# An encoder block on one core: the second half of its last gate as one product of 1024 columns, three of its eight pieces by seven products

## The chip, the cores and the metric

The kernel runs on 1 core of one Trainium2 chip. The metric is the device time of one execution in microseconds (us); the time of a kernel is the median of its runs. Before the change three runs took 1457.73, 1457.87 and 1458.08 us.

## The reference, cut to what matters

The program is one layer of an encoder on 256 tokens of 2048 features, all in float32: a combined input projection, two kinds of attention, gates, an output projection, a gated MLP, and at the end an embedding `p` (256 x 256) that is projected and gated by the residual. The change touches the last three lines:

```python
    x = x + (jax.nn.gelu(g) * (hf @ w_ffn_up[i])) @ w_ffn_down[i]
    gate_p = jax.nn.sigmoid(rms_norm(x, ple_norm[i]) @ w_ple_gate[i])   # 2048 x 2048
    x = x + gate_p * (p[i] @ w_ple_proj[i])
    return rms_norm(x, final_norm)
```

The result is 256 x 2048. The last norm needs the sum of squares over all 2048 columns of a token before any of its columns can be scaled and written.

## The kernel before, in words

**Products in three parts.** Each float32 operand is held as a rounded part ("hi", type float32r) and a remainder ("lo"). One product of a 128 x 128 block of activations with 128 rows x 512 columns of weights is three matmuls, hi·hi, hi·lo and lo·hi (`thirds`, L361, lines L364 to L366), summed in one PSUM bank. PE (TensorE) does them; the activations are the stationary side.

**Pieces.** All weights come as pieces of 1 MB (128 x 2048 elements) in the order in which PE will use them; the table `_PIECES` is written once by `_pieces` (L109). SP (SyncE) loads them in that order into 3 buffers (`load`, L240). `produce` (L246) turns a piece into units: ACT (ScalarE) copies hi from the raw weights (L263), DVE (VectorE) subtracts to get lo (L264). hi and lo units lie in rings of buffers, 6 for plain units ("u") and 2 for summed ones ("v", L184); a unit is made when a ring has a buffer free, that is when PE has used up an older one.

**Two ways to use a piece.** A piece of a 1024-column product holds two rows of blocks (k and k+1) by two column groups of 512; with the two halves of the tokens (t = 0, 1) that is a 2 x 2 times 2 x 2 block product. Kind "s" takes it by 8 products (24 matmuls) in two units of 1024 columns. Kind "S" takes it by 7 products (21 matmuls), into the banks M1, M7, M5, M6, M2, M3, M4. For that it needs sums of the activations (`combos`, tiles S, made once and kept) and of the weights: DVE writes three differences into the raw piece (L256 on 1024 columns, L257 and L258 on 512), and the piece becomes four units: 512 and 1024 plain columns (u) and two of 1024 summed columns (v; T13 from the first half of the raw piece, T24 from the second). Before the last piece of such a stage, `row_sums` (L803) combines M1, M6, M7 and M5 into two tiles c0 and c1 (one copy on ACT, L810, and four adds on DVE, L811 to L814); each finished output bank (M2, M3, M4, P22) is then added to them by DVE.

**The end of the program.** After the MLP's last product (stage F11) come pp0 and pp1 (`p` times its weights, kept in the tile `last`), then the last gate in three stages. G0 is its first 1024 columns: eight pieces in the pattern "SsSsSsSs" (`ALT`); its outputs go through `first_rows` and `ple` (L1077, L1068): add c, tanh on ACT (L1071), times the projection (DVE, L1072), plus the residual xr (DVE, L1073), square with a row sum (ACT, L1074), times the norm's weights (DVE, L1075). G2 and G3 are the third and fourth 512 columns, each by `wide_stage` (L421): four pieces by 8 products, in two accumulators, one for each half of the tokens. In G3 the last two pieces are joined, first all products of t = 0, then all of t = 1, so that the rows of t = 0 are finished and written while PE works on t = 1. What follows the last matmul is in L1091 to L1110: on halves of 256 columns tanh (L1094), times the projection (L1095), plus the residual (L1096), square (L1097); then the row sum (L1099, L1100), its power -1/2 on POOL (GpSimd, L1102), the norm's weights (L1103), the scaling of four column groups (L1109 on DVE, L1107 on ACT) and the transfer of each (L1110).

The norm's weights `gains` (1 MB, L1035) are loaded by SP right after the MLP in the program's order.

**What sets the order.** The kernel is written in program order with steps that fall due at a place (stage, piece, product). A scheduling layer then writes one fixed order for each engine; each engine runs its own in that order and waits on semaphores. Buffers are handed on in the order in which they are asked for.

Of the kernel before, what the change touches and what calls it, by code (L numbers as in the profile page):

```python
# [12 lines left out]
AF = mybir.ActivationFunctionType  # L13
# [4 lines left out]
T = 256  # L18
# [75 lines left out]
ALT = "SsSsSsSs"  # L94
DOWN = "SsSsSsSsSss"
FIRST_GATES = "ssssSsSs"


def _ffn(half):
# [10 lines left out]
def _pieces():  # L110
# [77 lines left out]
def _encoder(ctx: ExitStack, tc, xt, pt, xrow, cols, gainrow, table, onehot, mask, ident_in, wts, out):  # L188
# [92 lines left out]
    def drop(u):  # L281
        del made[u]
        state["u" if _UNITS[u][1] == "n" else "v"] += 1
        pump()
# [518 lines left out]
    def row_sums(stage, last, finish):  # L803

        names = ("M2", "M3", "M4", "P22")

# [17 lines left out]
    def quads(stage, moving, combos, finish):  # L824
        last = len(_STAGES[stage]) - 1
        row_sums(stage, last, finish)
        quad_stage(stage, moving, combos)
        run_due(stage, last, 8)

    def sums_of(u, tag):  # L830

# [203 lines left out]
    nc.sync.dma_start(gains, gainrow)  # L1035
    for pair, which in enumerate(("M2", "M3", "M4", "P22")):
        at(("pp0", 0, 4 + pair), rows_pair, which, 4 + pair, pl, 2)

# [41 lines left out]
        ple(t, n, c, c)  # L1080

    quads("G0", lambda k: pl[:, k, :], lambda i: combos["pl", i], first_rows)
    c = outputs()
    for a, t in zip(wide_stage("G2", lambda k: pl[:, k, :], ("M1", "M7")), range(2)):
        ple(t, 2, a, c[t][:, cut[0]])
    accs = wide_stage("G3", lambda k: pl[:, k, :], ("M5", "M6"), 2)
    known = sc.tile([P, 2], F32, name="known", bufs=1)
    nc.vector.tensor_reduce(known, ssq[:, :, :3], axis=AX.X, op=ALU.add)
    nc.vector.tensor_scalar(known, known, D * EPS, None, op0=ALU.add)
    for t in range(2):  # L1090
        for h in range(2):  # L1091
            cols = slice(3 * WIDE + h * T, 3 * WIDE + (h + 1) * T)
            u, r = c[t][:, WIDE + h * T:WIDE + (h + 1) * T], xr[:, t, cols]
            nc.scalar.activation(u, accs[t][:, h * T:(h + 1) * T], AF.Tanh, scale=held["rp"][:, t:t + 1])  # L1094
            nc.vector.scalar_tensor_tensor(u, u, 1.0, ph[:, t, cols], op0=ALU.add, op1=ALU.mult)  # L1095
            nc.vector.tensor_tensor(r, r, u, op=ALU.add)  # L1096
            nc.scalar.activation(u, r, AF.Square, accum_out=ssq[:, t, 3 + h:4 + h])  # L1097
        v = sc.tile([P, 1], F32, name="v3")
        nc.vector.tensor_tensor(known[:, t:t + 1], known[:, t:t + 1], ssq[:, t, 3:4], op=ALU.add)  # L1099
        nc.vector.tensor_scalar(v, ssq[:, t, 4:], known[:, t:t + 1], 1.0 / D, op0=ALU.add, op1=ALU.mult)  # L1100
        r = sc.tile([P, 1], F32, name="r3")
        nc.gpsimd.tensor_tensor(r, v, mhalf[:, :1], op=ALU.pow)  # L1102
        nc.vector.tensor_tensor(xr[:, t, cut[3]], xr[:, t, cut[3]], gains[:, cut[3]], op=ALU.mult)  # L1103
        for n in range(4):
            row = xr[:, t, cut[n]]
            if n == 1:
                nc.scalar.activation(row, row, AF.Copy, scale=r)  # L1107
            else:
                nc.vector.tensor_scalar(row, row, r, None, op0=ALU.mult)  # L1109
# [55 lines left out]
```

## Time and profile before

| what | us |
|---|---|
| median of three runs | 1457.87 |
| the profiled execution | 1458.43 |
| its span | 1456.6 |
| PE busy | 1445.2 |
| DVE busy | 1248.2 |
| ACT busy | 824.1 |

The span is that of the profiler, and the profiled execution took 1.83 us more than its span; it lies 0.56 us above the median. Engines are named as above; a DMA that SP or ACT starts is listed under SPq or ACTq. A matmul's shown length (0.39 us at 512 columns) is longer than the step from one to the next, because matmuls overlap; the step is what counts. In a row of the order in time the number in brackets is how long the engine had been idle, and for whom.

### The profile page before, as it was taken

How to read it: one execution, taken by the hardware profiler on the slowest of the kernel's cores; microseconds unless marked ns; L12 is line 12 of the kernel's file. 1: busy time of each engine (PE TensorE's matmuls, PEld its weight loads, DVE VectorE, ACT ScalarE, POOL GpSimd, SP SyncE). 2: the span in 40 equal slices, each digit the busy share in tenths (PEclk: the TensorE clock that was granted, in tenths of full speed). 3: DMA queues.
4: the chain of work that ended last, by engine and by line, in shares of the span. 5: the costliest groups of instructions: out<-in, count | busy, mean ns of one | idle time of the engine just before them, and what ended most of it. 6: DMA issues, size and time to landing. Idle time of an engine off the chain costs nothing.

```text
span 1456.6 us, 19524 instructions
## 1 busy us (share of the span) xinstructions
PE 1445.2 (99%) x7488; PEld 1237.1 (85%) x7488; DVE 1248.2 (86%) x1841; ACT 824.1 (57%) x1149; POOL 4.9 (0%) x9
## 2 busy tenths in 40 slices
PE   9999999999999999999999999999999999999997
PEld 8888888888888888888888888888888888888785
DVE  7777665679998989989888899989888889999994
ACT  7555544546555656566555555455555555565763
POOL 0000000000000000000000000000000000000000
PEclk9999999999999999999999999999999999999999
DMA  9764445435456456465554545465555554546462
GB/s 319 259 205 152 148 170 175 174 143 202 187 192 233 185 204 238 177 231 190 188 200 175 202 149 224 173 257 182 201 181 195 182 195 172 191 193 249 156 233 85
DMA packets 46456, 282.88 MB, mean 194 GB/s; under 512 B 5076, under 2 KB 9812, under 8 KB 14108
## 3 DMA queue, kind: packets, MB, share of 16 engines
q1 hardware_dynamic: 45500, 280.46, 52.7%
q8 instruction: 58, 0.95, 0.3%
q10 hardware_dynamic: 864, 1.19, 0.2%
q14 instruction: 34, 0.28, 0.1%
HBM read 279.49 MB, written 2.14 MB: 193 GB/s over the span
## 4 chain that ended last, share of the span: by engine, by line
PE 98%; ACT 1%; issue 0%; DMA 0%; DVE 0%; POOLq 0%; POOL 0%; ACTq 0%; DVEq 0%
PE bank L307 29%; PE bank L314 15%; PE bank L364 14%; PE bank L365 14%; PE bank L366 14%; PE bank L291 2%; PE bank L353 2%; PE bank L355 2%; PE bank L354 2%; PE bank L292 1%; PE bank L858 1%; PE bank L675 0%; PE bank L623 0%; PE bank L622 0%; PE bank L621 0%
## 5 line engine op out<-in xcount | busy, mean ns | idle before, releaser
L263 ACT ACTIVATE uh<-raw 128x1024 fp32r<-128x1024 f32 (+2 forms) x518 | 522.1, 1017 | 402.2 <-PE bank L307 183.4
L264 DVE TENSOR_TENSOR ul<-raw,uh 128x1024 fp32r<-128x1024 f32 (+2 forms) x518 | 596.6, 1169 | 134.1 <-ACT uh L263 70.3
L307 PE MATMUL bank<-hf,uh 128*128 128x512 f32 x1408 | 336.4, 391 | 0.0
L307 PEld LDWEIGHTS bank<-hf,uh 128*128 128x128 f32 x1408 | 258.9, 188 | 50.2
L314 PEld LDWEIGHTS bank<-hf,ul 128*128 128x128 f32 x1408 | 180.4, 191 | 6.7
L314 PE MATMUL bank<-hf,ul 128*128 128x256 f32 x1408 | 182.8, 283 | 0.0
L263 ACT ACTIVATE vh<-raw 128x1024 fp32r<-128x1024 f32 x92 | 97.4, 1059 | 55.7 <-DVE raw L256 27.9
L264 DVE TENSOR_TENSOR vl<-raw,vh 128x1024 fp32r<-128x1024 f32 x92 | 111.8, 1218 | 0.4
L307 PE MATMUL bank<-hs,uh 128*128 128x512 f32 x432 | 103.6, 392 | 0.0
L445 ACT ACTIVATE t<-bank 128x256 f32<-128x256 f32 x122 | 46.5, 384 | 95.1 <-PE bank L314 89.7
L307 PEld LDWEIGHTS bank<-hs,uh 128*128 128x128 f32 x432 | 79.5, 188 | 15.6
L364 PE MATMUL bank<-uh,act 128*128 128x512 f32 x232 | 90.4, 390 | 0.0
L365 PE MATMUL bank<-ul,act 128*128 128x512 f32 x232 | 90.4, 390 | 0.0
L366 PE MATMUL bank<-uh,act 128*128 128x512 f32 x232 | 90.3, 389 | 0.0
L364 PE MATMUL bank<-uh,hs 128*128 128x512 f32 x172 | 67.3, 391 | 0.0
L366 PE MATMUL bank<-uh,hs 128*128 128x512 f32 x172 | 67.2, 391 | 0.0
L365 PE MATMUL bank<-ul,hs 128*128 128x512 f32 x172 | 67.1, 390 | 0.0
L256 DVE TENSOR_TENSOR raw<-raw 128x1024 f32<-128x1024 f32 x46 | 56.1, 1220 | 0.6
L314 PE MATMUL bank<-hs,ul 128*128 128x256 f32 x432 | 56.6, 284 | 0.0
L314 PEld LDWEIGHTS bank<-hs,ul 128*128 128x128 f32 x432 | 54.5, 191 | 1.0
L364 PE MATMUL bank<-vh,S 128*128 128x512 f32 x138 | 54.3, 398 | 0.0
L365 PE MATMUL bank<-vl,S 128*128 128x512 f32 x138 | 54.1, 392 | 0.0
(240 smaller groups left out, 2275.1 us busy)
## 6 DMA issues: line engine op xcount, KB each, us to landing
raw<-in_wts SPq DMA_DIRECT2D x251, 1024.0 KB, 4.8
raw<-in_wts SPq DMA_DIRECT2D x12, 512.0 KB, 7.3
xr<-in_xrow SPq DMA_DIRECT2D x4, 512.0 KB, 9.5
x<-in_xt SPq DMA_DIRECT2D x13, 128.0 KB, 6.5
hb<-hold SPq DMA_DIRECT2D x3, 514.0 KB, 7.5
hb<-hold SPq DMA_DIRECT2D x2, 768.0 KB, 7.4
last<-in_gainrow SPq DMA_DIRECT2D x1, 1024.0 KB, 4.9
out<-xr SPq DMA_DIRECT2D x4, 256.0 KB, 2.6
```

The lines of the kernel that those rows point to most:

```text
L256: nc.vector.tensor_tensor(raw[:, :2 * WIDE], raw[:, WIDE:3 * WIDE], raw[:, :2 * WIDE], op=ALU.subtract)
L263: nc.scalar.activation(hi, src, AF.Copy)
L264: nc.vector.tensor_tensor(lo, src, hi.bitcast(F32), op=ALU.subtract)
L291: nc.tensor.matmul(acc, hi[:, w], m, start=first, stop=False, skip_group_check=True)
L307: nc.tensor.matmul(acc, weights(u)[0][:, o * P:(o + 1) * P], m, start=first, stop=False, skip_group_check=True)
L314: nc.tensor.matmul(acc[:, T:], weights(u)[1][:, o * P:(o + 1) * P], m[:, :T], start=False, stop=last, skip_group_check=True)
L353: nc.tensor.matmul(acc[:, :n * P], xh, hi, start=(k == 0), stop=False)
L354: nc.tensor.matmul(acc[:, :n * P], xh, lo, start=False, stop=False)
L364: nc.tensor.matmul(acc, sh, wh, start=first, stop=False)
L365: nc.tensor.matmul(acc, sh, wl, start=False, stop=False)
L366: nc.tensor.matmul(acc, sl, wh, start=False, stop=last)
L445: keep(nc.scalar.activation(t, acc[:, T:], AF.Copy, scale=scale))
```

## The change

G2 and G3 become one stage G2 over the last 1024 columns, in eight pieces of the pattern `LAST = "SsSsSsss"`: pieces 0, 2 and 4 (counted from 0) by seven products, the others by eight. The sums of the activations for pieces 0, 2 and 4 are those that G0 made. The last two pieces are joined: PE takes them output by output, (t, n) = (0,0), (0,1), (1,0), (1,1), with 12 matmuls for each, n being the column group. The combining of M1, M6, M7 and M5 falls due one piece earlier, at piece 5.

Each output goes through `last_rows` when its bank is done: add c (DVE, L1101), tanh (ACT, L1102), times the projection (DVE, L1103), plus the residual (DVE, L1104), square (ACT, L1106). The last output, (1,1), is taken in two halves of 256 columns. When n = 1 is done, the row's power is formed and the row of that t is scaled and written. For t = 0 two column groups are scaled by ACT (L1125), and two by DVE with the norm's weights in the same instruction (L1129), where there were a multiplication (L1103) and three scalings on DVE before.

The load of `gains` moves from behind the MLP to the first product of G0. On SP it stood behind the load of F11's last piece and now stands after that of G0's piece 4, seven loads later.

```diff
+LAST = "SsSsSsss"
...
-    for s in (2, 3):
-        wide("G%d" % s, ("w_ple_gate", s * WIDE), KC)
+    quads("G2", ("w_ple_gate", 2 * WIDE), ("w_ple_gate", 3 * WIDE), LAST)
...
-    def quad_stage(stage, moving, combos=None, tags=("M2", "M3", "M4", "P22")):
+    def quad_stage(stage, moving, combos=None, tags=("M2", "M3", "M4", "P22"), joint=1):
...
-        for i, p in enumerate(pieces):
+        alone = len(pieces) - joint if joint > 1 else len(pieces)
+        for i, p in enumerate(pieces[:alone]):
...
+        rest = [(i, c) for i in range(alone, len(pieces)) for c in range(2)]
+        for g, (t, n, i, c) in enumerate((t, n, i, c) for t in range(2) for n in range(2) for i, c in rest):
+            run_due(stage, alone, g)
+            w = cut(_UNITS_OF[pieces[i]][c], n if c == 0 else 1 - n)
+            put(tags[2 * t + n], part(moving(2 * i + c), t), w)
+        for i, c in rest:
+            drop(_UNITS_OF[pieces[i]][c])
...
-        at((stage, last, 0), first)
+        at((stage, last, 0) if joint == 1 else (stage, last - 1, 0), first)
         for t in range(2):
             for n in range(2):
-                at((stage, last, 2 * (2 * t + n + 1)), end, t, n)
+                at((stage, last, 2 * joint * (2 * t + n + 1)), end, t, n)
...
-    nc.sync.dma_start(gains, gainrow)
+    at(("G0", 0, 0), lambda: keep(nc.sync.dma_start(gains, gainrow)))
...
+    def last_rows(t, n, a):
+
+        end = 3 * WIDE if n else 2 * WIDE
+        step = T if t and n else WIDE
+        for h in range(WIDE // step):
+            cols = slice(end + h * step, end + (h + 1) * step)
+            u, r = held["c"][t][:, cols.start - 2 * WIDE:cols.stop - 2 * WIDE], xr[:, t, cols]
+            nc.vector.tensor_tensor(u, a[:, h * step:(h + 1) * step], u, op=ALU.add)
+            nc.scalar.activation(u, u, AF.Tanh, scale=held["rp"][:, t:t + 1])
             nc.vector.scalar_tensor_tensor(u, u, 1.0, ph[:, t, cols], op0=ALU.add, op1=ALU.mult)
             nc.vector.tensor_tensor(r, r, u, op=ALU.add)
-            nc.scalar.activation(u, r, AF.Square, accum_out=ssq[:, t, 3 + h:4 + h])
+            e = 2 + n + h
+            nc.scalar.activation(u, r, AF.Square, accum_out=ssq[:, t, e:e + 1])
+        k = known[:, t:t + 1]
+        if not n:
+            nc.vector.tensor_reduce(k, ssq[:, t, :3], axis=AX.X, op=ALU.add)
+            nc.vector.tensor_scalar(k, k, D * EPS, None, op0=ALU.add)
+            if t:
+                nc.vector.tensor_tensor(xr[:, t, cut[2]], xr[:, t, cut[2]], gains[:, cut[2]], op=ALU.mult)
+            return
         v = sc.tile([P, 1], F32, name="v3")
...
+        for m in range(4):
+            row = xr[:, t, cut[m]]
+            if m == 1 or not (t or m):
                 nc.scalar.activation(row, row, AF.Copy, scale=r)
+            elif t or m < 2:
+                nc.vector.tensor_scalar(row, row, r, None, op0=ALU.mult)
             else:
-                nc.vector.tensor_scalar(row, row, r, None, op0=ALU.mult)
-            (nc.scalar if n % 2 else nc.sync).dma_start(out[:, t, cut[n]], row)
+                nc.vector.scalar_tensor_tensor(row, row, r, gains[:, cut[m]], op0=ALU.mult, op1=ALU.mult)
+            (nc.scalar if m % 2 else nc.sync).dma_start(out[:, t, cut[m]], row)
+
+    quads("G2", lambda k: pl[:, k, :], lambda i: combos["pl", i], last_rows, 2)
```

Three places in the engines' orders show what this moves. The first is DVE where it makes the third piece of the stage after G0 (raw_12679 in both kernels). Before, the rows stand among the last steps for G0's outputs, and all the lo units (ul) are of plain weights:

```order
L1073 TENSOR_TENSOR xr_4920<-xr_4920,c_12721 128x512
L264 TENSOR_TENSOR ul_12772<-raw_12679,uh_12771 128x1024
L1075 TENSOR_TENSOR xr_4920<-xr_4920,last_12302 128x512
L264 TENSOR_TENSOR ul_12776<-raw_12679,uh_12775 128x1024
L1079 TENSOR_TENSOR c_12721<-bank_12520,c_12721 128x512
L264 TENSOR_TENSOR ul_12810<-raw_12692,uh_12809 128x1024
L264 TENSOR_TENSOR ul_12820<-raw_12692,uh_12819 128x1024
L1072 SCALAR_TENSOR_TENSOR c_12721<-c_12721,last_12302 128x512
```

Now, on the same engine from the second plain unit of that piece (ul_12787) to its last summed unit (vl_12833):

```order
L264 TENSOR_TENSOR ul_12787<-raw_12679,uh_12786 128x1024
L1083 TENSOR_TENSOR xr_4920<-xr_4920,last_12302 128x512 x2
L1087 TENSOR_TENSOR c_12732<-bank_12520,c_12732 128x512
L256 TENSOR_TENSOR raw_12679<-raw_12679 128x1024
L1080 SCALAR_TENSOR_TENSOR c_12732<-c_12732,last_12302 128x512
L257 TENSOR_TENSOR raw_12679<-raw_12679 128x512
L1081 TENSOR_TENSOR xr_4920<-xr_4920,c_12732 128x512
L258 TENSOR_TENSOR raw_12679<-raw_12679 128x512
L264 TENSOR_TENSOR vl_12813<-raw_12679,vh_12812 128x1024
L1083 TENSOR_TENSOR xr_4920<-xr_4920,last_12302 128x512
L264 TENSOR_TENSOR vl_12833<-raw_12679,vh_12832 128x1024
```

The three differences and the two summed units of the piece now stand between the steps for G0's last output. From the lo half of the first unit of G0's last piece (ul_12648, which stands at the same place in both orders) to vl_12833 DVE has 39 instructions: 13 of 1024 columns and 26 of 512.

The second place is DVE at the end of the program. Before, from the first use of the rows' power of t = 0 (r3_13053) the rows of t = 1 follow by themselves:

```order
L1109 TENSOR_SCALAR xr_4920<-xr_4920,r3_13053 128x512 x3
L1095 SCALAR_TENSOR_TENSOR c_12786<-c_12786,last_12302 128x256 x2
L1096 TENSOR_TENSOR xr_4920<-xr_4920,c_12786 128x256 x2
L1099 TENSOR_TENSOR known_13039<-known_13039,ssq3_12442 128x1
L1100 TENSOR_SCALAR v3_13072<-ssq3_12442,known_13039 128x1
L1103 TENSOR_TENSOR xr_4920<-xr_4920,last_12302 128x512
L1109 TENSOR_SCALAR xr_4920<-xr_4920,r3_13075 128x512 x3
```

Now, from the add of output (1,0) (bank_12828) to the first instruction for the last output's halves after tanh (bank_12864 is the last output):

```order
L1101 TENSOR_TENSOR c_12985<-bank_12828,c_12985 128x512
L1117 TENSOR_SCALAR v3_13051<-ssq3_12441,known_12796 128x1
L1129 SCALAR_TENSOR_TENSOR xr_4920<-xr_4920,r3_13053,last_12302 128x512 x2
L1103 SCALAR_TENSOR_TENSOR c_12985<-c_12985,last_12302 128x512
L1101 TENSOR_TENSOR c_12985<-bank_12864,c_12985 128x256
L1104 TENSOR_TENSOR xr_4920<-xr_4920,c_12985 128x512
L1101 TENSOR_TENSOR c_12985<-bank_12864,c_12985 128x256
L1109 TENSOR_REDUCE known_12796<-ssq3_12441 128x1
L1112 TENSOR_TENSOR xr_4920<-xr_4920,last_12302 128x512
L1110 TENSOR_SCALAR known_12796<-known_12796 128x1
L1103 SCALAR_TENSOR_TENSOR c_12985<-c_12985,last_12302 128x256 x2
L1104 TENSOR_TENSOR xr_4920<-xr_4920,c_12985 128x256 x2
```

The scaling of t = 0 and most of output (1,0) now stand ahead of the add of the last output.

The third place is ACT there, where c_12985 is the tile of t = 1. Before:

```order
L1107 ACTIVATE xr_4920<-xr_4920,r3_13053 128x512
L1110 DMA out_0<-xr_4920 128x512 x2
L1094 ACTIVATE c_12786<-bank_12934,rh_12388 128x256 x2
L1097 ACTIVATE c_12786,ssq3_12442<-xr_4920 128x256 x2
L1107 ACTIVATE xr_4920<-xr_4920,r3_13075 128x512
```

Now:

```order
L1102 ACTIVATE c_12985<-c_12985,rh_12387 128x512
L1125 ACTIVATE xr_4920<-xr_4920,r3_13053 128x512 x2
L1130 DMA out_0<-xr_4920 128x512 x2
L1106 ACTIVATE c_12985,ssq3_12441<-xr_4920 128x512
L1102 ACTIVATE c_12985<-c_12985,rh_12387 128x256 x2
L1106 ACTIVATE c_12985,ssq3_12441<-xr_4920 128x256 x2
L1125 ACTIVATE xr_4920<-xr_4920,r3_13108 128x512
```

The square of output (1,0) stands ahead of the last output's tanh.

More of the change, by code (lines that the diff above doesn't have):

```diff
@@ L801, in outputs, with row_sums @@
         return held["c"]
-    def row_sums(stage, last, finish):
+    def row_sums(stage, last, finish, joint=1):
         names = ("M2", "M3", "M4", "P22")
@@ L817, in end, with quads @@
             finish(t, n, held["accs"][names[2 * t + n]])
-        at((stage, last, 0), first)
+        at((stage, last, 0) if joint == 1 else (stage, last - 1, 0), first)
         for t in range(2):
             for n in range(2):
-                at((stage, last, 2 * (2 * t + n + 1)), end, t, n)
[L824 to L828, printed above, removed]
+                at((stage, last, 2 * joint * (2 * t + n + 1)), end, t, n)
+    def quads(stage, moving, combos, finish, joint=1):
+        last = len(_STAGES[stage]) - joint
+        row_sums(stage, last, finish, joint)
+        quad_stage(stage, moving, combos, joint=joint)
+        run_due(stage, last, 8 * joint)
     def sums_of(u, tag):
@@ L1082, in _encoder @@
     quads("G0", lambda k: pl[:, k, :], lambda i: combos["pl", i], first_rows)
[L1083 to L1086, printed above, removed]
     known = sc.tile([P, 2], F32, name="known", bufs=1)
[L1088 to L1094, printed above, removed]
+    def last_rows(t, n, a):
[6 more added lines that the diff above has]
+            nc.scalar.activation(u, u, AF.Tanh, scale=held["rp"][:, t:t + 1])
@@ L1098, in _encoder @@
         v = sc.tile([P, 1], F32, name="v3")
-        nc.vector.tensor_tensor(known[:, t:t + 1], known[:, t:t + 1], ssq[:, t, 3:4], op=ALU.add)
-        nc.vector.tensor_scalar(v, ssq[:, t, 4:], known[:, t:t + 1], 1.0 / D, op0=ALU.add, op1=ALU.mult)
+        if t:
+            nc.vector.tensor_tensor(k, k, ssq[:, t, 3:4], op=ALU.add)
+        nc.vector.tensor_scalar(v, ssq[:, t, 3 + t:4 + t], k, 1.0 / D, op0=ALU.add, op1=ALU.mult)
         r = sc.tile([P, 1], F32, name="r3")
         nc.gpsimd.tensor_tensor(r, v, mhalf[:, :1], op=ALU.pow)
-        nc.vector.tensor_tensor(xr[:, t, cut[3]], xr[:, t, cut[3]], gains[:, cut[3]], op=ALU.mult)
@@ L1104, in _encoder @@
-        for n in range(4):
-            row = xr[:, t, cut[n]]
-            if n == 1:
+        if t:
+            nc.vector.tensor_tensor(xr[:, t, cut[3]], xr[:, t, cut[3]], gains[:, cut[3]], op=ALU.mult)
+        for m in range(4):
+            row = xr[:, t, cut[m]]
+            if m == 1 or not (t or m):
                 nc.scalar.activation(row, row, AF.Copy, scale=r)
-            else:
-                nc.vector.tensor_scalar(row, row, r, None, op0=ALU.mult)
-            (nc.scalar if n % 2 else nc.sync).dma_start(out[:, t, cut[n]], row)
+            elif t or m < 2:
+                nc.vector.tensor_scalar(row, row, r, None, op0=ALU.mult)
+            else:
+                nc.vector.scalar_tensor_tensor(row, row, r, gains[:, cut[m]], op0=ALU.mult, op1=ALU.mult)
+            (nc.scalar if m % 2 else nc.sync).dma_start(out[:, t, cut[m]], row)
```

## The prediction

> **What bounds the kernel now.** I read the page first, then the busy time by stages.
>
> ```profile
> span 1456.6 us, 19524 instructions
> PE 1445.2 (99%) x7488; PEld 1237.1 (85%) x7488; DVE 1248.2 (86%) x1841; ACT 824.1 (57%) x1149; POOL 4.9 (0%) x9
> PE 98%; ACT 1%; issue 0%; DMA 0%; DVE 0%; POOLq 0%; POOL 0%; ACTq 0%; DVEq 0%
> ```
>
> PE is the bound over the whole: fewer matmuls are worth their time, if PE is not made to wait. Whether it will is read from the stages. The rows are G0, then G2 with G3, then what follows the last matmul.
>
> ```profile
> core 0: us, PE busy (x) PEld busy (x) DVE busy (x) ACT busy (x) POOL busy (x), PEclk, DMA share, GB/s
> 1362.20:1403.00 40.80, 40.80 (x180) 33.44 (x179) 40.07 (x55) 24.08 (x30) 1.07 (x1) 1.00 0.56 214
> 1403.00:1446.95 43.95, 43.95 (x194) 36.04 (x193) 31.26 (x46) 21.99 (x37) 0.93 (x1) 1.00 0.29 105
> 1446.95:1456.60 9.65, 0.00 (x0) 0.00 (x0) 3.71 (x10) 2.47 (x7) 0.93 (x1) 0.68 0.57 211
> ```
>
> In G0, where every second piece goes by seven products, DVE is busy for 40.07 of 40.80 us: it only just keeps up. In G2 and G3 it has 12.7 us to spare, and the change puts DVE work there. In the waits from 1300 us on PE has one, for the copy of a pp output:
>
> ```profile
> PE bank L364 <- ACT last L1059: 0.6, 1, 0.6
> ```
>
> **PE's own work.** 49 matmuls in a row, the first and the last of them:
>
> ```profile
> 1435.68 0.39 PE L366 MATMUL bank<-uh,pl 128*128 128x512 f32 x1
> ...
> 1446.56 0.39 PE L366 MATMUL bank<-uh,pl 128*128 128x512 f32 x1
> ```
>
> One step is (1446.56 − 1435.68)/48 = 0.227 us. Three pieces by 21 matmuls in place of 24 save 9 x 0.227 = 2.04 us. From 1403.0 the 183 matmuls would put the start of the last one at 1444.5 instead of 1446.56.
>
> **The load of the norm's weights.** Before, SP held the following loads behind it; the rows are SP's wait, and then ACT and DVE without raw weights.
>
> ```profile
> SPq L1035 <- PE bank L366: 6.3, 1, 6.3
> ...
> 1340.67 2.01 ACT L263 ACTIVATE uh<-raw 128x1024 fp32r<-128x1024 f32 x2 [6.05 <-DMA raw<-in_wts]
> ...
> 1341.77 2.36 DVE L264 TENSOR_TENSOR ul<-raw,uh 128x1024 fp32r<-128x1024 f32 x2 [2.37 <-ACT uh L263]
> ```
>
> At its new place, behind the load of G0's piece 4, its buffer has long been free, and its first use (L1083) is over 30 us later; the loads behind it wait for DVE to empty a buffer anyway, so it costs nothing there. Freed of the 6.3 us, DVE starts the pp pieces earlier, by 0 to 2.4 us; the six u buffers, which PE empties, will take part of that back, and I take 1.0. PE's 0.6 us should mostly go too.
>
> **DVE's work at the hand-over from G0.** A piece by seven products needs three differences and 3584 columns of lo in place of 2048. The queue's price for 512 and 1024 columns:
>
> ```profile
> 1375.76 0.68 DVE L850 TENSOR_TENSOR pair<-pl 128x512 f32<-128x512 f32 x1
> 1376.36 0.68 DVE L264 TENSOR_TENSOR ul<-raw,uh 128x512 fp32r<-128x512 f32 x1
> ...
> 1391.85 1.22 DVE L264 TENSOR_TENSOR ul<-raw,uh 128x1024 fp32r<-128x1024 f32 x1
> 1392.98 1.22 DVE L264 TENSOR_TENSOR vl<-raw,vh 128x1024 fp32r<-128x1024 f32 x1
> 1394.12 3.52 DVE L264 TENSOR_TENSOR ul<-raw,uh 128x1024 fp32r<-128x1024 f32 x3
> ```
>
> From start to start 0.60 and 1.14 us, the last one of a chain its full 1.22. The differences add 1.14 + 2 x 0.60, the lo units (0.60 + 3 x 1.14) − 2 x 1.14 = 1.74: 4.1 us more for each of three pieces. The first of them meets the outputs of G0, on which DVE spends 16 instructions of 512 columns and four for the combining, none of which G0's own start had beside it.
>
> The row at 1391.85 is ul_12648, where the quoted order starts counting. From there to the end of vl_12833 stand 26 of 512 and 13 of 1024 columns: 26 x 0.60 + 12 x 1.14 + 1.22 = 30.5 us, so 1422.35 without a gap, and 1421.35 with the 1.0 us above. PE reaches vl_12833 in the third piece; from its first use to the end it has 117 matmuls. The last starts at 1421.4 + 116 x 0.227 = 1447.7. Until piece 4 the sums stay level: vl_12894 is ready at 1430.2 and wanted at 1430.25, so each gap of DVE (where it waits for a copy or a square of ACT) goes straight to the end. I add 0.4 for these, with bounds 0 and 1. The start of the last matmul moves from 1446.56 to 1448.1, **+1.5 us** (bounds +0.4 and +2.7). So of the 2.04 us nothing is left, and PE waits some 4 us in all, most of it in the third piece for the units made after L256 to L258 (about 2 us at one place, since the square of an output also stands ahead of the last hi copy on ACT).
>
> Here a rule bears on the price. The Trainium skill, "VectorE: DVE Perf Modes", section "The DRAIN you can't avoid", says that the next operation does not start until the pipe has emptied, which I read as: each costs its whole duration. Then the 39 would take 26 x 0.68 + 13 x 1.22 = 33.5 us and the end would be 3.0 us later. The rows above show starts 0.08 us before the predecessor's end, so the sum goes by 0.60 and 1.14.
>
> **The end of the program.** The rows are those of t = 0 and t = 1 before, with one square and one tanh of 512 columns from G2.
>
> ```profile
> 1406.58 0.61 ACT L1074 ACTIVATE c<-xr 128x512 f32<-128x512 f32 x1
> 1407.10 0.19 ACT L1074 ACTIVATION_READ_ACCUMULATOR c<-xr 128x1 f32 x1
> ...
> 1414.00 0.71 ACT L1071 ACTIVATE c<-c,rh 128x512 f32<-128x512 f32 x1
> ...
> 1441.12 0.39 PE L366 MATMUL bank<-uh,pl 128*128 128x512 f32 x1
> ...
> 1441.54 0.84 ACT L1094 ACTIVATE c<-bank,rh 128x256 f32<-128x256 f32 x2 [9.59 <-PE bank L366]
> ...
> 1444.15 0.21 DVE L1100 TENSOR_SCALAR v<-ssq,known 128x1 f32<-128x1 f32 x1 [0.24 <-ACT c L1097]
> 1444.45 0.93 POOL L1102 TENSOR_TENSOR r<-v,mhalf 128x1 f32<-128x1 f32 x1 [78.33 <-DVE v L1100]
> 1445.41 1.28 DVE L1109 TENSOR_SCALAR xr<-xr,r 128x512 f32<-128x512 f32 x3 [0.44 <-POOL r L1102]
> 1447.12 0.84 ACT L1094 ACTIVATE c<-bank,rh 128x256 f32<-128x256 f32 x2 [0.98 <-PE bank L366]
> 1447.62 0.79 DVE L1095 SCALAR_TENSOR_TENSOR c<-c,last 128x256 f32<-128x256 f32 x2 [0.94 <-ACT c L1094]
> ```
>
> Call L the start of the last matmul (1446.56). A bank is read 0.42 us after its last matmul starts (1441.12 to 1441.54), and from the row sum to its use is 1.26 us (1444.15 to 1445.41). Before, the last rows' product (L1095) starts at L + 1.06. Now output (0,1) is done 24 matmuls before the last: DVE adds at L − 5.0, tanh runs until L − 3.6, product and sum on DVE until L − 2.1 (the row sum of (0,0) in between waits for its square), its square until L − 1.25, the row sum starts at L − 1.2, and the power is there at about L. The new wait is that of L1129 for it. Behind it in DVE's queue stand the product and the sum of (1,0) and the add of the last output: L1129 twice until L + 1.25, product to 1.85, add of a half (0.35) to 2.2, sum of (1,0) ends at 2.9. Then ACT squares (1,0) until 3.65, before the last tanh; DVE waits for that row sum, multiplies by the norm's weights (0.60), and starts the last output's products at L + 4.45. From there the work is that of before (two products, two sums, two squares, power, four scalings, transfers). So the end grows by 4.45 − 1.06, **+3.4 us**. If L1129 did not wait, the add could come at L + 0.45 and the products at L + 3.1: at least +2.0; at most +4.0, with 0.6 more for gaps. I take 3.3.
>
> **The sum.** +1.5 + 3.3 = +4.8 us. In the profiled execution's own time 1458.43 + 4.8 = 1463.2; that execution lies 0.56 above the median, so the median becomes 1457.87 + 4.8 = 1462.7. The bounds add up to +2.4 and +6.7.
>
> **Rivals.** First, DVE keeps up. If freeing SP lets DVE run ahead by 4 us or more instead of 1.0, every summed unit is there when PE wants it. Then PE ends 2.04 + 0.6 us earlier, the end still grows by 3.3, and the time is 1458.5: not slower. For it speaks ACT, which in G0 is busy 24.08 of 40.80 us; against it DVE's 40.07 and the two v buffers, which let no summed unit be made more than one piece ahead. 0.14.
>
> Second, the clock. The waits of the third piece lie close together, and a long enough rest takes the clock down. The rows are after the last matmul:
>
> ```profile
> 1449.00:1450.00 1.00, 0.00 (x0) 0.00 (x0) 0.52 (x4) 0.69 (x4) 0.00 (x0) 1.00 0.53 201
> 1450.00:1451.00 1.00, 0.00 (x0) 0.00 (x0) 0.55 (x2) 0.01 (x1) 0.93 (x1) 0.67 0.00 0
> 1451.00:1452.00 1.00, 0.00 (x0) 0.00 (x0) 1.00 (x3) 0.71 (x1) 0.00 (x0) 0.50 0.00 0
> ```
>
> Some 3.5 us after PE's last work the granted clock is 0.50. If PE's 2 us grow to that, matmuls take 0.45 us for as long again: about 8 of them, 1.8 us, plus 1.5 of the longer wait, 1466.0. The Trainium skill, "TensorE: Matmul & The Clock Gate", section "Why this matters for your kernels", asks for no gap over about 3 us; the rows above agree with that size. 0.05.
>
> Third, the full pipe of the rule above: 3.0 us more, 1465.7. The rows speak against it. 0.03.
>
> **How the numbers follow.** The forecast has 0.78 (1460.3 to 1464.6 by its bounds). 0.2% is 2.9 us, about what a measurement of this kernel can tell from no change, so slower begins at 1460.8. Slower: 0.73 of the forecast and 0.08 of the last two, 0.81. Within 0.2%: 0.05 from its low end and 0.11 of the first rival, 0.16. Faster: 0.03, the first rival with a short end as well. The range of 1459.6 to 1465.2 leaves out most of the first rival at one side and the other two at the other.
>
> **What would show it.** In the new profile: no wait of 6.3 us on SP, DVE idle less than 2.37 us before the pp pieces, and PE's 0.6 us gone or smaller; DVE without a gap from G0's last pieces until about 1422; waits of PE of about 4 us on the v units in the third piece of the new stage; the last matmul starting at 1447 to 1449; L1129 starting at about L, the last L1103 at L + 4.45, and 13.4 us from L to the end of the span, against 10.0. I would be wrong if PE shows no wait in the new stage, or if the last tanh comes within 1 us of the last matmul.

## The result, and the profile after

| | before | after |
|---|---|---|
| median, us (6 runs each) | 1457.97 | 1463.73 |
| from, to | 1457.73 to 1458.43 | 1462.41 to 1464.74 |
| the profiled execution | 1458.43 | 1462.41 |
| its span | 1456.6 | 1460.6 |

The ratio is 1.0039, with a 95% interval of 1.0026 to 1.0052: the change makes the kernel slower by 5.76 us in the medians. The profiled execution of after is the fastest of its six, so its span shows less of the loss (4.0 us) than the medians do; where the rest comes from took experiments. Line numbers below are those of each kernel's own text; the edits shift them a little.

The page of after, in the same three lines as before:

```profile
span 1460.6 us, 19532 instructions
...
PE 1443.3 (99%) x7479; PEld 1233.3 (84%) x7479; DVE 1264.2 (87%) x1861; ACT 830.6 (57%) x1154; POOL 4.5 (0%) x9
...
PE 94%; DVE 3%; DMA 1%; issue 1%; ACT 1%; POOL 0%; POOLq 0%; ACTq 0%; DVEq 0%
```

The nine matmuls are gone (7488 to 7479) and PE is busy for 1.9 us less, but the chain that ends last now runs over DVE for 3% of the span where it had 0%. PE's waits from 1300 us on, where the one for the pp output was the only one before:

```profile
PE bank L364 <- ACT vh L263: 2.2, 2, 1.9
...
PE bank L365 <- DVE ul L264: 0.5, 1, 0.5
```

They are waits for units of the third piece of the new stage. PE's rows there, in order of time (start, length, and in brackets the idle time ahead):

```profile
1411.79 0.39 PE L364 MATMUL bank<-uh,S 128*128 128x512 f32 x1
1412.69 0.50 PE L365 MATMUL bank<-ul,pl 128*128 128x512 f32 x1 [0.51 <-DVE ul L264]
1413.02 0.40 PE L366 MATMUL bank<-uh,pl 128*128 128x512 f32 x1
...
1415.99 0.39 PE L364 MATMUL bank<-uh,pl 128*128 128x512 f32 x1
1416.72 0.73 PE L364 MATMUL bank<-vh,S 128*128 128x512 f32 x2 [0.34 <-ACT vh L263]
1419.33 0.50 PE L364 MATMUL bank<-vh,S 128*128 128x512 f32 x1 [1.88 <-ACT vh L263]
1419.67 0.39 PE L365 MATMUL bank<-vl,S 128*128 128x512 f32 x1
...
1420.58 0.39 PE L364 MATMUL bank<-vh,pl 128*128 128x512 f32 x1
1421.11 0.50 PE L365 MATMUL bank<-vl,S 128*128 128x512 f32 x1
1421.44 0.40 PE L366 MATMUL bank<-vh,S 128*128 128x512 f32 x1
```

The brackets undercount, since a matmul is drawn longer than its step. By starts less steps of 0.227 us the pauses are 0.90 − 0.23 = 0.67, 0.73 − 0.23 = 0.50, 2.61 − 0.45 = 2.16 and 0.53 − 0.23 = 0.30 us; the first step behind three of them takes 0.33 or 0.34 instead of 0.23 (1412.69 to 1413.02, 1419.33 to 1419.67, 1421.11 to 1421.44). Together that is about 4.0 us (3.63 of pauses and 0.32 in the slow first steps), against 2.04 us of matmuls saved.

What DVE did up to there: the lo units of pp0 and those of pp1, then the two ends of the chain that the prediction counted, ul_12648 and vl_12833.

```profile
1338.25 2.36 DVE L264 TENSOR_TENSOR ul<-raw,uh 128x1024 fp32r<-128x1024 f32 x2
...
1342.03 2.36 DVE L264 TENSOR_TENSOR ul<-raw,uh 128x1024 fp32r<-128x1024 f32 x2 [1.42 <-ACT uh L263]
...
1389.88 1.22 DVE L264 TENSOR_TENSOR ul<-raw,uh 128x1024 fp32r<-128x1024 f32 x1
...
1419.83 1.22 DVE L264 TENSOR_TENSOR vl<-raw,vh 128x1024 fp32r<-128x1024 f32 x1
```

Ahead of pp0, where DVE idled 2.37 us before, it does not idle now; 1.42 us of idle time stand ahead of pp1 instead, since ACT, which makes the hi units, waits there 1.77 us for PE to use up u buffers. So the load's early lead is taken back in part, as forecast. The 39 instructions of DVE end at 1421.05, 31.17 us after they began. PE's last matmul, POOL's and DVE's rows around it:

```profile
1447.59 0.39 PE L366 MATMUL bank<-uh,pl 128*128 128x512 f32 x1
```

```profile
1446.61 0.55 POOL L1119 TENSOR_TENSOR r<-v,mhalf 128x1 f32<-128x1 f32 x1 [82.46 <-DVE v L1117]
```

```profile
1447.19 1.42 DVE L1129 SCALAR_TENSOR_TENSOR xr<-xr,r,last 128x512 f32<-128x512 f32 x2 [0.67 <-POOL r L1119]
1448.53 0.68 DVE L1103 SCALAR_TENSOR_TENSOR c<-c,last 128x512 f32<-128x512 f32 x1
1449.13 0.42 DVE L1101 TENSOR_TENSOR c<-bank,c 128x256 f32<-128x256 f32 x1
...
1451.67 0.75 DVE L1103 SCALAR_TENSOR_TENSOR c<-c,last 128x256 f32<-128x256 f32 x2
...
1453.73 0.21 DVE L1117 TENSOR_SCALAR v<-ssq,known 128x1 f32<-128x1 f32 x1 [0.24 <-ACT c L1106]
...
1454.99 1.28 DVE L1127 TENSOR_SCALAR xr<-xr,r 128x512 f32<-128x512 f32 x3 [0.45 <-POOL r L1119]
```

By the 0.42 us of the prediction the last output's bank can be read from 1448.0 on, but DVE is at the scaling of t = 0 and then at (1,0), and adds it only at 1449.13. The last products start 4.08 us after the last matmul (1.06 before), and the span ends 13.01 us after it (10.04 before).

### The profile page after: what moved, and what is told of

Read it like the earlier page. It is cut to its first block, busy times and chain, and to the rows that moved or that the text cites. A ratio compares the mean times of both kernels' runs of the same rounds, so it can differ in the third digit from the quotient of the medians.

```text
span 1460.6 us, 19532 instructions
## 1 busy us (share of the span) xinstructions
PE 1443.3 (99%) x7479; PEld 1233.3 (84%) x7479; DVE 1264.2 (87%) x1861; ACT 830.6 (57%) x1154; POOL 4.5 (0%) x9
## 4 chain that ended last, share of the span: by engine, by line
PE 94%; DVE 3%; DMA 1%; issue 1%; ACT 1%; POOL 0%; POOLq 0%; ACTq 0%; DVEq 0%
PE bank L307 29%; PE bank L314 15%; PE bank L365 13%; PE bank L366 13%; PE bank L364 13%; PE bank L353 2%; PE bank L291 2%; PE bank L355 2%; PE bank L354 2%; PE bank L292 1%; DMA raw<-in_wts 1%; DVE ul L264 1%; PE bank L866 1%; PE bank L683 0%; PE bank L631 0%
## 5 line engine op out<-in xcount | busy, mean ns | idle before, releaser
L263 ACT ACTIVATE vh<-raw 128x1024 fp32r<-128x1024 f32 x98 | 103.6, 1058 | 59.8 <-DVE raw L256 29.2
L264 DVE TENSOR_TENSOR vl<-raw,vh 128x1024 fp32r<-128x1024 f32 x98 | 119.2, 1220 | 0.4
L256 DVE TENSOR_TENSOR raw<-raw 128x1024 f32<-128x1024 f32 x49 | 59.8, 1221 | 0.6
L364 PE MATMUL bank<-vh,S 128*128 128x512 f32 x147 | 57.6, 400 | 2.2 <-ACT vh L263 2.2
L365 PE MATMUL bank<-vl,S 128*128 128x512 f32 x147 | 57.8, 393 | 0.2
L366 PE MATMUL bank<-vh,S 128*128 128x512 f32 x147 | 57.3, 390 | 0.0
```

The source lines that it names most:

```text
L256: nc.vector.tensor_tensor(raw[:, :2 * WIDE], raw[:, WIDE:3 * WIDE], raw[:, :2 * WIDE], op=ALU.subtract)
L263: nc.scalar.activation(hi, src, AF.Copy)
L264: nc.vector.tensor_tensor(lo, src, hi.bitcast(F32), op=ALU.subtract)
L364: nc.tensor.matmul(acc, sh, wh, start=first, stop=False)
L365: nc.tensor.matmul(acc, sh, wl, start=False, stop=False)
L366: nc.tensor.matmul(acc, sl, wh, start=False, stop=last)
```

## The experiments

Before each number stands what was expected. The kernel before ran beside them on the same chip: 1458.60 us (1457.66 to 1459.43, 21 runs) for e1 to e4, 1458.59 us (1457.93 to 1459.23, 15 runs) for e5 to e8, one run of 1458.86 us for e9 to e12.

**e1_again: the kernel after once more.** No edit.

> The changed kernel once more, nothing edited; six runs of it lay between 1462.4 and 1464.7 us, and its profiled execution was the fastest. My theory (DVE late at the hand-over from G0, and the queue order at the end) expects a median of 1463.7 +- 0.7 and a profile in which the last matmul starts 1.0 us or more later than in the kernel before and the end takes 13.0 us from there. If a slower execution is caught, the theory says that the excess lies in the waits of the third piece of the last stage, where a load that lands later goes into the chain. The rival that the end itself varies (power, transfers) expects the same start of the last matmul and a longer rest.

Measured: 1464.73 us (1463.56 to 1465.09), ratio 1.0039 (1.0027 to 1.0052). The median lies above the 1463.0 to 1464.4 expected. The profiled execution took 1464.89 us, 2.5 us more than that of the result, and the excess is not in the waits, as the theory had it: PE's pauses in the third piece are the same; but then the granted clock falls. Busy times in stretches of 2 us (PE, PEld, DVE, ACT, POOL, granted clock, DMA share, GB/s), of e1 and below of after:

```profile
1420.00:1422.00 2.00, 1.49 (x6) 1.05 (x6) 2.00 (x3) 0.46 (x1) 0.00 (x0) 0.93 0.03 8
1422.00:1424.00 2.00, 2.00 (x5) 1.43 (x5) 2.00 (x3) 0.00 (x0) 0.00 (x0) 0.50 0.39 66
1424.00:1426.00 2.00, 2.00 (x7) 1.54 (x7) 2.00 (x3) 0.00 (x0) 0.00 (x0) 0.71 0.90 381
1426.00:1428.00 2.00, 2.00 (x10) 1.65 (x9) 1.97 (x3) 0.86 (x1) 0.00 (x0) 1.00 1.06 442
```

```profile
1422.00:1424.00 2.00, 2.00 (x11) 1.57 (x10) 2.00 (x4) 0.00 (x0) 0.00 (x0) 1.00 0.83 274
```

Five matmuls in 2 us instead of eleven: the rival of the clock has come about, in this execution and not in the other, behind a pause of 2.2 us (1.9 in the bracket) that did not grow. e9 to e12 return to it.

**e2_gains_alone: before, with only the load of the norm's weights moved.**

```diff
-    nc.sync.dma_start(gains, gainrow)
+    at(("G0", 0, 0), lambda: keep(nc.sync.dma_start(gains, gainrow)))
```

> The kernel before with only the load of the norm's weights moved to the first product of G0. My theory: SP's wait of 6.3 us and PE's 0.6 us at the pp copy go, PE has no other wait, so 1457.3 us (-0.6, between -1.0 and 0). The rival that the moved load is what costs in the change (it collides with the weights of G0) expects 1459 or more and waits of PE on loads in G0.

Measured: 1457.99 us (1457.15 to 1458.87, 11 runs), ratio 0.9996 (0.9987 to 1.0005). No wait of PE is listed from 1300 us on, and its last matmul:

```profile
1446.05 0.39 PE L366 MATMUL bank<-uh,pl 128*128 128x512 f32 x1
```

The span ends 10.05 us later, at 1456.1, as before. The moved load shows no cost. The median is 0.6 us lower, as expected, but the interval does not tell that from nothing.

**e3_gains_back: after, with the load at its old place.** The edit of e2 the other way round.

> The changed kernel with the load of the norm's weights back at its old place. My theory: DVE loses its lead again, the waits of the third piece stay, so the time is 0.5 to 1.5 us above the changed kernel (about 1464.7), and the end stays at 13.0 us. The rival that the moved load is what costs expects 1459 to 1460.5.

Measured: 1465.27 us (1463.29 to 1465.61), ratio 1.0042 (1.0029 to 1.0056). PE's wait ahead of G0 is back, the pauses of the third piece stay:

```profile
PE bank L364 <- ACT vh L263: 2.2, 2, 1.9
...
PE bank L364 <- ACT last L1067: 0.6, 1, 0.6
```

So the old place brings that wait back, and it has no part in the pauses. In the time 0.5 us is too little to be told apart here.

**e4_two_sevens: after, with two of the eight pieces by seven products**, with the first of the three left out, so that the first one left is the third piece behind G0.

```diff
-LAST = "SsSsSsss"
+LAST = "ssSsSsss"
```

> The changed kernel with the pattern ssSsSsss: the first piece behind G0 by eight products, so two pieces by seven. My theory: DVE gets through G0's outputs before the first differences, PE has no wait over 0.2 us in the last stage, its last matmul starts 6 x 0.227 + 0.6 = 2.0 us earlier than in the kernel before (1444.6), and the end still takes 13.0 us: 1458.9 us (1458.3 to 1460). The rival that pieces by seven products cost wherever they stand expects a third of the waits to go: about 1462.5.

Measured: 1460.85 us (1459.58 to 1461.38, 10 runs), ratio 1.0014 (1.0004 to 1.0023): 2.25 us above before, and more than expected. From 1300 us on no wait of PE is listed. Its last matmul, and DVE's scaling of t = 0:

```profile
1445.74 0.39 PE L366 MATMUL bank<-uh,pl 128*128 128x512 f32 x1
```

```profile
1445.62 1.42 DVE L1129 SCALAR_TENSOR_TENSOR xr<-xr,r,last 128x512 f32<-128x512 f32 x2 [0.66 <-POOL r L1119]
```

From the first matmul of G0 (1362.33) to the last are 83.41 us, in e2 84.74 (from 1361.31): 1.33 us less, which is the 6 matmuls x 0.227 us that two pieces save. Without those pauses a saved matmul is worth its whole time. The run both takes one piece's extra work from DVE and moves the first one away from G0's outputs; which of the two does it, three pieces by seven in another place would show, and that was not run. The end is longer than in after, 1459.1 − 1445.74 = 13.36 us, because the scaling of t = 0 begins 0.12 us before the last matmul and not 0.40. By these terms e2's 1457.99 − 1.33 + 3.31 gives 1459.97; 0.9 us stay open. About 0.4 of them lie outside the span: time less span is 2.1 to 2.2 us in e4's ten runs and 1.8 to 1.9 in e2's eleven. The rest may be the start of G0, which is 1.02 us later in e4's profile than in e2's, though the two programs have the same code up to there.

**e5_filled: after, with PE given work in place of the pauses**: 12 matmuls by zeros, which add nothing to the sums, behind the first product of the third piece.

```diff
+    zero = const.tile([P, 64], FR, name="zero")
+    nc.scalar.activation(zero, ones[:, :64], AF.Copy, scale=0.0)
...
+                    for _ in range({0: 12}.get(g, 0) if (stage, i) == ("G2", 2) else 0):
+                        tc.keep_in_program_order(nc.tensor.matmul(
+                            accs[name][:64], zero, moving(0), start=False, stop=False))
```

> The kernel after, with 12 matmuls by zeros (they add nothing to the sums) in PE's queue behind the first product of the third piece of the new stage: 12 x 0.227 = 2.7 us of work that PE does while it would otherwise wait. Theory: the time of the kernel after comes in two groups, about 1.3 us apart, since PE's pauses in the third piece let the granted clock fall afterwards in a part of the executions. With the pauses filled (the longest under 1.2 us) the clock stays at 1.00 until PE's end, the last matmul starts about 87 us after the first of G0 as in the profile without a fall, the executions lie within 1.5 us, and the median is the kernel before + 5.0 (4.4 to 5.4). Rival: the groups come from elsewhere in the program; then the median stays at the kernel before + 5.8 to 6.1 and the executions spread over 2 us. Third way: the zeros only push PE back, + 8.5.

Measured: 1463.91 us (1463.18 to 1465.44), ratio 1.0039 (1.0025 to 1.0052). PE's rows:

```profile
1412.68 2.90 PE L423 MATMUL bank<-pl,zero 128*64 128x512 f32 x12
...
1420.38 0.50 PE L366 MATMUL bank<-vh,S 128*128 128x512 f32 x1 [0.59 <-ACT vh L265]
```

One matmul more every 0.227 us for 2.7 us, and the last one of the program starts 86.90 us after the first of G0, not later than in after (87.29). That settles who sets the pace in this piece: DVE and ACT, and PE only waits. For the clock the times decide little. It stays at 1.00 in the profile and the median lies in the range given (before + 5.3), but the interval holds after's ratio as well, and the executions still spread over 2.26 us, against the 1.5 expected.

**e6_one_pause: after, with one unit late**, so that PE rests once for long instead of several times. The hi copy of T13 of the third piece is made three times.

```diff
-        nc.scalar.activation(hi, src, AF.Copy)
+        for _ in range(3 if p == _STAGES["G2"][2] and kind == "T13" else 1):
+            nc.scalar.activation(hi, src, AF.Copy)
```

> The kernel after, with the hi copy of the first summed unit of the third piece made three times by ACT (the same values): the unit comes two copies of about 0.95 us later, and PE's order of the piece changes so that, by the durations in the profile, the pauses of 0.5 and 2.2 us become one of about 3.1 us, the sum of the pauses and the start of the last matmul staying within 0.3 us. Theory (a pause lets the clock fall): the granted clock falls to 0.5 in nearly every execution, the executions no longer lie in two groups, and the median is the kernel before + 6.8 (6.3 to 7.5). Rival (the clock has no part in it): the kernel before + 5.8 to 6.1, as the kernel after, in the same two groups.

Measured: 1464.86 us (1463.52 to 1465.96), ratio 1.0044 (1.0032 to 1.0057), before + 6.3, the low end of what was expected. The pauses did become one:

```profile
1416.94 0.40 PE L365 MATMUL bank<-uh,pl 128*128 128x512 f32 x1
1420.33 0.50 PE L366 MATMUL bank<-ul,pl 128*128 128x512 f32 x1 [3.00 <-DVE ul L265]
```

That execution is the fastest of the five, and its clock stays at 1.00 through a rest of 3.39 us from start to start. "Nearly every execution" was thus wrong for the only one seen in a profile. Of the other four, at 1464.52 to 1465.96, only the mean granted clock is on record: 0.996, where the profiled one has 0.997.

**e9_look, e10_look (after) and e11_pause_look, e12_pause_look (e6): four more profiles**, to see whether the time goes with the clock.

> The kernel after once more, for one profile. Theory (in a part of the executions the granted clock falls behind the pauses of the third piece and costs 1.3 us): if the granted clock is below 0.95 anywhere between 1420 and 1428, the last matmul starts 88.2 us or more after the first of G0; if it stays at 1.00, 87.2 to 87.4 us. Rival: the distance does not go with the clock.

> As the look before: 88.2 us or more from the first matmul of G0 to the last one with a fall of the granted clock between 1420 and 1428, 87.2 to 87.4 us without one. Rival: the distance does not go with the clock.

> The kernel of e6 (one pause of 3 us) once more, for one profile. Theory: its executions of 1464.5 and above are those with a fall of the granted clock behind the pause; with a fall the distance from the first matmul of G0 to the last is 88.3 us or more, and without one 87.2 to 87.4 us, as in the profile of e6. Rival: the distance is 87.3 us either way, and the slower executions lose their time elsewhere.

> As the look before: 88.3 us or more with a fall of the granted clock behind the pause, 87.2 to 87.4 us without one. Rival: 87.3 us either way.

The clock falls in e9, e11 and e12, not in e10. The two stretches of e11 behind its one pause:

```profile
1420.00:1422.00 2.00, 1.68 (x4) 1.39 (x5) 2.00 (x4) 1.22 (x2) 0.00 (x0) 0.51 0.00 0
1422.00:1424.00 2.00, 2.00 (x7) 1.52 (x7) 2.00 (x3) 0.00 (x0) 0.00 (x0) 0.64 0.04 8
```

The profiles with the three pieces by seven products and the pauses unfilled, and the others below them (us; G0 is the start of its first matmul, L that of the last):

| profile | time | G0 | L | L − G0 | clock falls |
|---|---|---|---|---|---|
| after | 1462.41 | 1360.30 | 1447.59 | 87.29 | no |
| e3_gains_back | 1463.29 | 1361.26 | 1448.44 | 87.18 | no |
| e6_one_pause | 1463.52 | 1361.45 | 1448.70 | 87.25 | no |
| e7_scaling_last | 1462.85 | 1361.42 | 1448.66 | 87.24 | no |
| e10_look | 1464.60 | 1362.64 | 1449.76 | 87.12 | no |
| e1_again | 1464.89 | 1361.67 | 1450.07 | 88.40 | yes |
| e9_look | 1464.78 | 1361.80 | 1449.96 | 88.16 | yes |
| e11_pause_look | 1464.88 | 1361.47 | 1450.04 | 88.57 | yes |
| e12_pause_look | 1466.15 | 1362.63 | 1451.34 | 88.71 | yes |
| e5_filled | 1463.29 | 1361.57 | 1448.47 | 86.90 | no |
| before | 1458.43 | 1362.15 | 1446.56 | 84.41 | no |
| e2_gains_alone | 1457.90 | 1361.31 | 1446.05 | 84.74 | no |
| e4_two_sevens | 1461.20 | 1362.33 | 1445.74 | 83.41 | no |
| e8_two_and_end | 1460.04 | 1362.15 | 1445.64 | 83.49 | no |

Without a fall the distance is 87.12 to 87.29 us in five profiles, with one 88.16 to 88.71 in four (e9's is 0.04 and e10's 0.08 below what was expected). Against the profiles with the same pauses a fall costs 1.2 us (e1) and 1.0 (e9), and behind the single pause 1.3 (e11) and 1.5 (e12). The loss lies behind the pause: from the first matmul after the long pause to the last one are 28.26 us in after and 28.32 in e10, but 29.56 in e1 and 29.39 in e9. But e10 takes 1464.60 us without a fall: its G0 starts at 1362.64. So the executions differ for two reasons, the clock and a start of G0 that varies between 1360.3 and 1362.6 us in these profiles. My theory for e5, which put all of the spread on the clock, was half of it. Why G0's start varies was not tried.

**e7_scaling_last: after, with the scaling of t = 0 behind the last output's products, sums and squares.**

```diff
+        if t and n:
+            held["late"](keep)
...
-        for m in range(4):
+        def scale(pin=lambda ins: ins):
+            for m in range(4):
...
+        if t:
+            scale()
+        else:
+            held["late"] = scale
```

> The kernel after, with the scaling of t = 0 (L1129 on DVE, the two copies on ACT, and their transfers) behind the last output's products, sums and squares. Theory (DVE's wait for POOL and its two scalings stand ahead of the last output): the last products start 2.4 us after the last matmul instead of 4.1, the span ends 12.0 us after it instead of 13.0, and the median is the kernel before + 4.8 (4.3 to 5.3). Rival: at the end DVE's work as a whole, or the transfers of t = 0 that now come late, set the end; then the order is worth nothing, + 5.8 to 6.1, or the end is later still.

Measured: 1463.30 us (1462.57 to 1463.72), ratio 1.0032 (1.0020 to 1.0045), before + 4.7. DVE's rows of the last products, the scaling of t = 0 and the last row sum:

```profile
1451.00 0.75 DVE L1103 SCALAR_TENSOR_TENSOR c<-c,last 128x256 f32<-128x256 f32 x2
...
1452.33 1.41 DVE L1132 SCALAR_TENSOR_TENSOR xr<-xr,r,last 128x512 f32<-128x512 f32 x2
...
1454.33 0.21 DVE L1119 TENSOR_SCALAR v<-ssq,known 128x1 f32<-128x1 f32 x1
```

L is 1448.66, so the last products start at L + 2.34 instead of L + 4.08, as expected (2.4). But the span ends at L + 12.44, not 12.0: DVE's scaling now stands ahead of the last row sum, which comes at L + 5.67 against L + 6.14 in after (1453.73 − 1447.59). Of the 1.74 us gained at the products 0.47 are left there, and 0.57 at the end. Half of the theory holds: the order matters, and DVE's work as a whole matters too. The median of after lay 5.76 and 6.13 us above before in its two sets of runs; of the 1.0 to 1.4 us less here the end explains 0.57.

**e8_two_and_end: e4, with less of that work ahead of the last row sum.** DVE's two scalings of t = 0 stand behind it, (1,0) is squared behind the last tanh, and the norm's weights of t = 1 go into the last scalings instead of two multiplications of their own.

```diff
-            nc.scalar.activation(u, u, AF.Tanh, scale=held["rp"][:, t:t + 1])
+            pin(nc.scalar.activation(u, u, AF.Tanh, scale=held["rp"][:, t:t + 1]))
...
+            if t and n:
+                held["square"](keep)
...
-        if t:
-            nc.vector.tensor_tensor(xr[:, t, cut[3]], xr[:, t, cut[3]], gains[:, cut[3]], op=ALU.mult)
+        if t:
+            held["late"](keep)
...
-            elif t or m < 2:
+                elif m < 2:
...
+            scale(of=range(2))
+            held["late"] = lambda pin: scale(pin, range(2, 4))
```

> The kernel with two pieces by seven products (that of e4), and its end in another order: DVE's two scalings of t = 0 behind the last row sum, the square of (1,0) behind the last tanh, and the products by the norm's weights of (1,0) and (1,1) made within the last scalings. Theory (the added end is DVE's and ACT's order, not the transfers): the last products start about 2.1 us after the last matmul, the span ends 11.5 us after it instead of 13.4, and the median is the kernel before + 0.5 (-0.3 to + 1.2), from + 2.2 for e4. Rival: the transfers set the end, since those of t = 0 and t = 1 now come close together; then the end stays at over 12.7 us and the time at + 1.6 or more.

Measured: 1459.36 us (1458.76 to 1460.04, 11 runs), ratio 1.0005 (0.9996 to 1.0014): before + 0.8, and 1.5 less above before than e4. DVE's rows:

```profile
1447.83 0.42 DVE L1111 SCALAR_TENSOR_TENSOR c<-c,last 128x256 f32<-128x256 f32 x1 [0.43 <-ACT c L1103]
...
1450.13 0.21 DVE L1136 TENSOR_SCALAR v<-ssq,known 128x1 f32<-128x1 f32 x1
...
1451.98 1.41 DVE L1149 SCALAR_TENSOR_TENSOR xr<-xr,r,last 128x512 f32<-128x512 f32 x2
```

With L at 1445.64 the last products start at L + 2.19 and the row sum at L + 4.49 instead of 6.14. The last scaling ends at L + 7.75, in after at L + 8.68; the span ends at L + 12.36, 1.0 us before e4's, but not at the 11.5 expected. One part of the miss shows: POOL's last power took 0.99 us beside DVE's scalings, where in e7, with DVE idle, it took 0.55. Neither this nor any other of these kernels is measurably faster than before; e2 and e8 cannot be told from it.

## Why the prediction was right, and where it was not

The direction and the mechanism of the two main terms were right: 1462.7 was forecast, 1463.73 measured. Step by step:

- **PE's own work**, −2.04 us: right. The counts differ by 9, and e4 against e2 gives 1.33 us for 6, which is 0.222 us for one.
- **The load of the norm's weights**: right. SP's wait and PE's 0.6 us are gone, DVE idles 0.95 us less in sum ahead of pp0 and pp1 (1.0 taken), and e2 and e3 show nothing else that hangs on it.
- **The hand-over**, +1.5: a little too small. The chain on DVE took 31.17 us, 30.5 + 0.67 of gaps, where I had added 0.4. Read between the profiles without a fall, L − G0 grew from 84.74 (e2) to about 87.2, +2.5; less the 0.6 of pp that is +1.9, within the bounds. In the profile of the result L moved only by +1.03 (1446.56 to 1447.59), since that execution had reached G0 early (1360.30). The pauses sum to 4.0 us, as forecast, and 2.16 of them stand at one place. e5 shows them to be DVE's and ACT's.
- **The full pipe**: the rule from the Trainium skill, "VectorE: DVE Perf Modes", section "The DRAIN you can't avoid", as I had read it, made the chain 33.5 us; it took 31.17. The same section adds that a next operation which is not held starts earlier. I had left that out, and the rows, with starts 0.08 us before the predecessor's end, agree with it.
- **The end**, +3.3: 13.01 − 10.04 = +2.97. The place was right. L1129 began at L − 0.40, not at L, because POOL's power took 0.55 us and not the 0.93 of the row that I had used; so the last products came at L + 4.08 instead of 4.45. In that row DVE works beside POOL (a multiplication by the norm's weights); in the new order DVE only waits for the power, which the prediction's own order shows. e7 shows what I had not seen: taking that wait away gives 1.74 us at the products and only 0.57 at the end, since DVE's total up to the last row sum is nearly as long.
- **The clock** is the step that failed. I made it hang on the pause growing to 3.5 us, at a chance of 0.05. It fell in two of four profiles of after, with the pause unchanged, and cost 1.0 to 1.2 us there, less than the 1.8 that I had put on it. The 3.5 us came from one trace's end; over the 14 profiles the clock falls between 2.4 and 5.7 us after the start of the last matmul.
- **The sum.** Terms as measured: −0.6 + 2.5 + 3.0 = +4.9 us without a fall, and nearer +6 with one; the medians of the two sets of runs lie 5.8 and 6.1 above before. That +4.9 is so near to the +4.8 of the forecast is in part luck: the hand-over was 0.4 us too small and the end 0.3 too large. How often the clock falls shows in the mean granted clock that is on record for every execution: 0.997 in the five profiles of the table's upper part without a fall, e7's among them, and 0.995 or 0.996 in the four with one. By it the clock fell in 5 of 13 executions of after (their median is 1464.8 us, that of the others 1463.6), in 6 of 7 of e6's kernel and in none of e5's five. This is an indication only, since the figure is rounded and holds the end of the program too. What is left of the medians, some tenths of a microsecond, stays open.

## What to carry to other kernels

Work taken from an engine that is busy all the time is worth its full price only while the units that feed it are early: count the feeding engine's instructions from the hand-over on, because there the old stage's outputs and the new stage's extra work meet. Leaving out the first of the three costlier pieces (e4), the one next to the hand-over, removed these pauses. At the end of a program list all that stands in the queue between the last result and the transfers, not only the wait that shows; when one wait is taken away, look at which total is next. And where PE pauses, add up the pauses that lie within any 3.4 us, not only the longest: here 2.2 us together were enough to halve the clock.

## What the runs showed of the hardware

**The clock is set at the edges of windows.** The clock's fall has a fixed length. From the rows of e1, the share lost is (0.07 + 0.50 + 0.29) x 2 us, which at half speed is 3.44 us; the times of the change that the traces keep give 3.41 us in all four. When it begins varies: in e1 PE had worked again since 1420.51 when the clock fell at 1421.73, in e11 it fell at 1420.04, still within the rest. The fall behind the pause and the one after the program's last matmul lie 30.72 us apart in e1 and 34.13 in e9, e11 and e12, which is 9 and 10 times 3.413 us. So in a trace without a fall at the pauses the one at the end shows where the edges lie.

Take as idle what is over 0.228 us from one matmul's start to the next, and add it up in each window of 3.413 us. In the 14 profiles no window with up to 2.08 us of idle time was followed by a fall (2.05 at the pauses of e3, e7 and e10, 2.08 at the end of e2), and every one that began at full speed and had 2.16 us or more was (in e1 2.18 at the pauses and 2.16 at the end; 2.48 in e12, 2.64 in e9, 2.88 in e11). That is why the same pauses of 0.5 and 2.2 us led to a fall in e1 and e9 and not in after and e10, and why a single rest of 3.39 us did in e11 and not in e6, where an edge cuts it into 1.99 and 1.42 us. An estimate from the traces without a fall: with the edges anywhere, the pauses of after reach 2.16 us in about half of the positions, the rest of e6 in seven tenths, and the pauses of e5 (1.13 us at most) and e4 in none. The reading was made after the runs, and none was made to test it.

The Trainium skill, "TensorE: Matmul & The Clock Gate", section "What's actually happening", tells of a window of about 3.4 us that runs freely and is not set by the kernel's start; the traces agree, with 3.413 us. Its advice in "Why this matters for your kernels", no gap over about 3 us, is not strict enough for these runs: pauses of at most 2.2 us were enough in e1 and e9.

**POOL's power beside DVE.** At the end of the 14 profiles the power of one number per row took 0.55 us where DVE was idle or busy for under 0.2 us beside it (13 times), and 0.92 to 0.99 us where DVE worked for 0.5 us or more beside it (15 times). Why was not tried.
